# A hybrid decoder step whose weights stream through TensorE: where its side work stands between the weight jobs

## The chip, the core and the metric

The kernel runs on one core of one Trainium2 chip. The metric is the device time of one execution in microseconds (us), as a median over runs. A profiler recorded one further execution, and every duration below comes from that record. Its engines are called PE (TensorE matmul), PEld (TensorE's weight load, which runs beside PE), DVE (VectorE), ACT (ScalarE), POOL (GpSimd) and SP (SyncE, which here only issues DMAs).

## What is computed

One inference step of a one-layer trunk, for 256 prompt tokens and 8 x 4 sample tokens together, 288 columns in all:

```python
x = layer_norm(x)                                   # 2048 features
a_h, a_bg, a_cg, qkv, z, beta, dec, c_u, c_v, gates = split_cols(x @ w_in)
out_a = (a_bg * causal_dwconv(a_cg * a_h)) @ w_a_out
o     = gated_delta_rule(q, k, v, g, beta, state)   # 8 heads, 128 x 128, from silu(conv(qkv))
out_b = (rms_norm(o) * silu(z)) @ w_b_out
out_c = (gelu(c_u) * chunk_spatial_mix(layer_norm(gelu(c_v)))) @ w_c_out
merged = sig(g0) * out_a + sig(g1) * out_b + sig(g2) * out_c
x   = layer_norm(ALPHA * x + merged @ w_o)
ffn = (silu(causal_dwconv(x @ w_up_g)) * (x @ w_up_u)) @ w_down
ple = sigmoid(x @ w_pg) * (p @ w_pe)
y   = layer_norm(ALPHA * x + ffn + ple)
```

The new convolution and delta-rule states are outputs as well. All is float32.

## The kernel before

**Weights and jobs.** All weight matrices are cut into 128 x 128 tiles and laid into one list in the order of use. Eight tiles are a *job*, one 512 KB DMA (`raw`, line 56). ACT copies a job to the rounded type fp32r (`wh`, line 74), DVE subtracts to get the rest (`wl`, line 81), and for each tile PE makes three matmuls of 288 columns (lines 212 to 214): high part of the activations by `wh`, their low part by `wh`, their high part by `wl`. The activations are held as a high and a low part too (`XH` and `XL`, and pairs like it). The list has 614 jobs. `Stream.next` hands out the tiles; when a job starts it runs, in this order, one piece of side work (`pump`), the DMA of a later job, the split of the job two ahead (`wh` on ACT, `wl` on DVE), and then the evacuations that fell due (`post`). In the middle of a job it calls `half`.

**Side work.** `later(fn, lag)` puts a function on a list that `pump` takes from, one per job. If that list is empty, `pump` advances a Python generator, `delta()`, by one step; `delta` is the gated delta rule. A step ends at a `yield`. A plain `yield` means that the next step starts at the next job's start. `yield 1` means that the next step may already run at the coming half. While the q, k and v columns are produced, a job that starts with such an evacuation skips its step. `staged` holds second halves of evacuations, run by the next `post`. `drain()` runs the evacuations, the list and then the generator to its end at once.

**The order of units** (a unit is one 128-row output): c_v, c_u (16 jobs each), q/k/v (48), gate 2 with `wc` (48), mixer A (48), gate 0 with `wa` (48), then `drain()`, z (16 jobs, from job 224), gate 1 with `wb`, `wo`, `wpe`, `wpg`, `wup`/`wdn` twice, and the output norm.

**Inside `delta()`**, for each of four groups of two heads: a step A transposes k, q and v to tokens (line 757) and makes their norms (`ss`, and `rr` by POOL). A step B makes the decays: three DVE operations `dec`, `decT`, `dec`, two exponentials on ACT. It ends with `yield 1`. Step C is one DVE operation, `kh` = k times `rr`. Step D transposes `kh` (line 782). Later a small triangular inverse goes to DRAM (`td`, line 826) and comes back in another shape by four DMAs into a buffer that the trace calls U (line 831). Four steps later DVE makes from it the tiles `T` and `U`, which the next step's matmuls (line 847) read. After the four groups come two passes for the samples, in which `kvd` goes to DRAM and back (line 1055), `son` is scaled, and PE transposes it (line 1074).

**`first()`** begins a run of units on a freshly normalised input: it goes over the 16 slices of features, and for each slice over four or eight accumulators, while `feed` makes the next slices' `XH` and `XL`. It is used for c_v at the start (4 accumulators) and for the first eight `wpg` units (8 accumulators, so that one slice is one job). For `wpg`, each accumulator's evacuation is a sigmoid on ACT into a buffer `u` (four buffers), and `fin`, three DVE operations (`M` times `u`, `t` = `XH` + `XL`, `M` + ALPHA `t`), which a `post()` runs at once.

**At the start** PE makes 40 matmuls on zeros (`warm`, line 255, tile `wz`) while the input arrives and is normalised. The first job is split in two halves (`split0`), lines 456 and 457; `ln.piece(1)` normalises features 512 to 1023 (`yt`, line 128) on DVE.

Of the kernel before, what the change touches and what calls it, by code (L numbers as in the profile page):

```python
# [18 lines left out]
KD = 16  # L19
# [81 lines left out]
def body(tc, I, O):  # L101
# [15 lines left out]
    def tt(out, a, b, op):  # L117
        V.tensor_tensor(out=out, in0=a, in1=b, op=op)  # L118

    def stt(out, a, s, b, op0, op1):  # L120
        V.scalar_tensor_tensor(out=out, in0=a, scalar=s, in1=b, op0=op0, op1=op1)  # L121
# [13 lines left out]
    def mid(ap, n):  # L135
        return ap.unsqueeze(1).to_broadcast([ap.shape[0], n, ap.shape[1]])
# [11 lines left out]
    def acc():  # L148
        return accp.tile([P, 512], F32, name="acc", tag="acc")

    def bank():
        return bgp.tile([P, 512], F32, name="bank", tag="bank")

    def t288(tag, bufs, pl=None):
        return (pl or tmp).tile([P, NT], F32, name=tag, tag=tag, bufs=bufs)

    def short():
        return t288("t", 6)

    def held():  # L160
        return t288("u", 4)

    st = Stream(nc, rawp, whp, wlp, I["wall"], 5, 2)
    deferred = []
    background = [None]
    posted = []
    staged = []
# [4 lines left out]
    def later(fn, lag=1):  # L172
        deferred.append((st.started + lag, fn))

    def pump():
        if deferred:
            if st.started >= deferred[0][0]:
                deferred.pop(0)[1]()
        elif background[0] is not None and not (heavy[0] and pace[0]):
            step()  # L180
# [11 lines left out]
    def flush():  # L192
        post()
        while deferred:
            deferred.pop(0)[1]()

    def drain():
        flush()
        while background[0] is not None:
            pump()  # L200
# [5 lines left out]
    X = (XH, XL)  # L206

    def mm3(key, pair, k, a, start, stop):
        wh, wl = st.next(key)
        xh, xl = pair[0][:, k, :], pair[1][:, k, :]  # L210
        o = a[:, 0:NT]
        PE.matmul(o, lhsT=wh, rhs=xh, start=start, stop=False)  # L212
        PE.matmul(o, lhsT=wh, rhs=xl, start=False, stop=False)  # L213
        PE.matmul(o, lhsT=wl, rhs=xh, start=False, stop=stop)  # L214

    def unit(name, m, pair, nk, evac, k0=0, now=False, a=None):
        a = acc() if a is None else a
        for k in range(nk):
            mm3((name, m, k0 + k), pair, k, a, k == 0, k == nk - 1)
        if now or len(st.order) % JT:  # L220
            evac(a)
        else:
            posted.append(lambda: evac(a))
            heavy[0] = name == "win" and m[0] in (C_QKV, C_QKV + 1024, C_QKV + 2048)

    def post(everything=True):
        late = staged[:]
        staged.clear()
        for f in late:
            f()  # L230
        while posted:
            posted.pop(0)()
        heavy[0] = False
        if everything and staged:
            post()
# [3 lines left out]
    def split_to(hl, i, y):  # L239
        copy(hl[0][:, i, :], y)  # L240
        tt(hl[1][:, i, :], y, hl[0][:, i, :].bitcast(F32), ALU.subtract)
# [10 lines left out]
    def warm(n, w=None):  # L252
        w = bank() if w is None else w
        for _ in range(n):
            PE.matmul(w, lhsT=wz[:, 0:P], rhs=wz, start=True, stop=True)

    def cv(i, n=1):
        return cvec[:, i:i + n]
# [85 lines left out]
    def feed(ln, off, k):  # L344
        if 0 <= k + 2 < KD:
            ln.s3(k + 2, off)
        if 0 <= k + ln.lead < KD and k + ln.lead not in ln.p:
            ln.s1(k + ln.lead, off)
        if 0 <= k + ln.lead - 1 < KD:
            ln.s2(k + ln.lead - 1, off)  # L350

    def first(names, ln, off, evacs, func):
        accs = [acc() if i < 4 else bank() for i in range(len(names))]
        st.late = True
        for k in range(KD):
            if k == KD - 4:
                st.late = False
            if k == KD - 2:
                A.preload_act_table(func)
            for a, (n, m), e in zip(accs, names, evacs):  # L360
                mm3((n, m, k), X, k, a, k == 0, k == KD - 1)
                if k == KD - 1:
                    e(a)
                    if len(names) > 4:
                        post()
            if k in (2, 6):
                ln.piece((k + 6) // 4)
            feed(ln, off, k)
# [46 lines left out]
    for j in range(2):  # L415
        s = BLK[j][0]
# [8 lines left out]
    for j in range(1, 4):  # L425
        st.dma(j)
    nc.sync.dma_start(out=cvec[:, 32:V_N], in_=I["cvec"][:, 32:V_N])
    warm(40)
    xs = M[0:NTS].rearrange("p k t -> p (k t)")[:, 0:16 * P]
    nm = const.tile([NTS, 2], F32, name="nm")  # L430
    A.activation(out=xs, in_=ln.yt[0:NTS, 2, :], func=AF.Identity, scale=-1.0 / 2048, accum_out=nm[:, 0:1])
# [22 lines left out]
    def split0(i):  # L454
        c = slice(i * 4, i * 4 + 4)
        A.activation(out=h0[:, c, :], in_=r0[:, c, :], func=AF.Copy)
        V.tensor_tensor(out=l0[:, c, :], in0=r0[:, c, :], in1=h0[:, c, :].bitcast(F32), op=ALU.subtract)
# [36 lines left out]

    for k in range(-ln.lead, 0):
        feed(ln, V_LNI, k)
        if k == -3:
            split0(1)
        if k == -2:
            st.split(1)  # L500
            ln.piece(1)
    st.subs()
    first([("win", (C_CV, m)) for m in range(4)], ln, V_LNI, [cv_evac(m) for m in range(4)], AF.Gelu_apprx_tanh)
    lstack.close()
    vln.pad(G)
# [175 lines left out]
    def delta():  # L681
# [39 lines left out]
        def D(tag, dt=F32, n=4):  # L721
            return dp.tile([P, n, P], dt, name=tag, tag=tag)
# [16 lines left out]
        for g in range(4):  # L739
# [33 lines left out]
            tt(Dm, Dm, mid(mk["mbS"], 4), ALU.add)  # L773
            A.activation(out=dT, in_=dT, func=AF.Exp)
            A.activation(out=Dm, in_=Dm, func=AF.Exp, scale=-1.0)
            yield 1
            kh = D("kh")
            tt(kh, kb, last(rr[:, 0:4], P), ALU.mult)
            yield
# [51 lines left out]
                nc.sync.dma_start(out=ex[:, u], in_=td[8 * u:8 * u + 8])  # L831
            yield 1
            yield 1
            yield 1
            yield 1
            U, T = D("U", F32R), D("T", F32R)
            for m, X2 in enumerate((T, U)):
                tt(X2.rearrange("p u (r c) -> p u r c", c=16),
# [1 line left out]
                   bd4.rearrange("p u (r c) -> p u r c", c=16), ALU.mult)  # L840
            B = D("B", F32R)
            G.tensor_tensor(out=B, in0=L, in1=mid(mk["m16"], 4), op=ALU.mult)
            yield
            for s in (16, 32, 64):
                w = b4(bank())
# [33 lines left out]
            for c in range(2):  # L879
                us = (c, 2 + c)  # L880
                if c:
# [4 lines left out]
                    for hh, u in enumerate(us):  # L886
                        h = 2 * g + hh
# [16 lines left out]
                else:  # L904
                    S2 = D("S2", n=2)
                    for hh in range(2):
                        h = 2 * g + hh
# [63 lines left out]
        for p in range(2):  # L971
# [7 lines left out]
            tt(Dm, Dm, mk["mbS4"], ALU.add)  # L979
            A.activation(out=dT, in_=dT, func=AF.Exp)  # L980
            A.activation(out=Dm, in_=Dm, func=AF.Exp, scale=-1.0)
            yield 1
            kb = bank()
            for i, src in enumerate((ks, qs, vs)):
                PE.transpose(kb[:, i * P:(i + 1) * P], src, ident)
# [67 lines left out]
            G.memset(kv3[3 * NTS:P], 0.0)  # L1053
            for i in range(3):
                G.dma_start(out=kv3[i * NTS:(i + 1) * NTS], in_=kvd.rearrange("(h t) d -> t h d", t=NTS))
            yield 1
            w = bank()
            PE.matmul(w[:, 0:P], lhsT=dT, rhs=vn, start=True, stop=True)
            tt(on, on, w[:, 0:P], ALU.add)
# [31 lines left out]
            for hl in range(4):  # L1091
                h = 4 * p + hl
# [17 lines left out]
        ds.close()  # L1110

    background[0] = delta()
    next(background[0])

# [60 lines left out]
        unit("win", (C_G, m), X, KD, gate_evac(gs))  # L1175
        unit("wa", m, YB, H, out_acc(m))

    drain()
    ng = cv(V_NB)

    def z_evac(h):
        def e(a):
            sz = held()
            A.activation(out=sz, in_=a[:, 0:NT], func=AF.Silu)
            y = short()
            stt(y[:, 0:NTP], QF[:, h, :], ng, sz[:, 0:NTP], ALU.mult, ALU.mult)
            stt(y[:, NTP:NT], SF[:, 0, h, :], ng, sz[:, NTP:NT], ALU.mult, ALU.mult)
            split_to(YB, h, y)
        return e

    for h in range(H):
        unit("win", (C_Z, h), X, KD, z_evac(h))
    post()
    astack.close()
# [20 lines left out]
    Y = l1p.tile([P, KD, NT], F32, name="Y")  # L1215
# [151 lines left out]

    def pg_evac(m):
        def e(a):
            s = held()  # L1370
            A.activation(out=s, in_=a[:, 0:NT], func=AF.Sigmoid)

            def fin():
                tt(M[:, m, :], M[:, m, :], s, ALU.mult)
                t = short()
                tt(t, XH[:, m, :].bitcast(F32), XL[:, m, :].bitcast(F32), ALU.add)
                stt(M[:, m, :], t, ALPHA, M[:, m, :], ALU.mult, ALU.add)
            staged.append(fin)
        return e

    first([("wpg", m) for m in range(8)], ln1, V_LN1, [pg_evac(m) for m in range(8)], AF.Sigmoid)
    l1stack.close()
    gstack.close()
    ystack.close()
    for m in range(8, KD):
        unit("wpg", m, X, KD, pg_evac(m))

    fstack = ExitStack()
    fp = pool(fstack, "fp")
# [196 lines left out]
```

## Time and profile before

| | |
|---|---|
| median of 3 runs | 2123.72 us (2121.94 to 2125.68) |
| profiled execution: its own time, its span | 2124.1 us, 2122.3 us |
| granted TensorE clock, mean over the span | 0.996 |
| PE busy | 2095.5 us, 99% |
| DVE busy | 1221.9 us, 58% |
| ACT busy | 961.2 us, 45% |
| POOL busy | 231.5 us, 11% |
| DMA | 346.37 MB, mean 163 GB/s; the main queue takes 46.7% of 16 engines' span |

Times in the trace count from the start of the span. A row of the timeline has the start, the duration, the engine, the line of the code, the operation, output and inputs, shape and count. The bracket at its end says how long the engine stood idle just before, and which engine's work let it go on. The table of waits sums those brackets.

### The profile page before, as it was taken

The page shows a single profiled execution, that of the slowest core. Times are in us where ns is not written, and L with a number is a line of the kernel's source. Part 1 is how long each engine was busy: PE and PEld are TensorE (multiplying, and loading weights), DVE is VectorE, ACT ScalarE, POOL GpSimd, SP SyncE. Part 2 cuts the span into 40 slices and gives each one's busy share as a digit, 9 for nine tenths or more (in the row PEclk, how much of TensorE's full clock was granted, in tenths as well). Part 3 has the DMA queues.
Part 4 walks back from the last instruction along what each step waited for, and adds up shares of the span by engine and source line. Part 5 has one row for each costly group of instructions (what it writes and reads, how often), then busy time and mean ns, then how long its engine had stood idle before and what let it go on. Part 6 is the DMA issues. An engine that isn't in the chain of part 4 may idle for free.

```text
span 2122.3 us, 38082 instructions
## 1 busy us (share of the span) xinstructions
PE 2095.5 (99%) x15708; PEld 2078.4 (98%) x15708; DVE 1221.9 (58%) x1761; ACT 961.2 (45%) x1470; POOL 231.5 (11%) x446
## 2 busy tenths in 40 slices
PE   9999999999999999999999999999999999999998
PEld 8999999999999999999999999999999999999998
DVE  6757866566565556545577565555544455555444
ACT  6446544343434445443445634444433344444333
POOL 2112321001101122000000201111100011111000
PEclk9999999999999999999999999999999999999999
DMA  6454544444345466454544444445454454544542
GB/s 241 144 169 159 165 158 143 152 139 154 124 153 183 139 214 213 161 171 162 189 159 149 160 149 166 167 162 169 161 168 163 165 168 162 168 163 165 167 160 105
DMA packets 101533, 346.37 MB, mean 163 GB/s; under 512 B 16352, under 2 KB 16912, under 8 KB 101200
## 3 DMA queue, kind: packets, MB, share of 16 engines
q1 hardware_dynamic: 97888, 331.90, 46.7%
q0 software_dynamic: 3472, 12.05, 1.8%
q8 instruction: 123, 2.02, 0.4%
q14 instruction: 50, 0.41, 0.1%
HBM read 335.22 MB, written 8.67 MB: 162 GB/s over the span
## 4 chain that ended last, share of the span: by engine, by line
PE 93%; DVE 3%; issue 2%; ACT 1%; POOL 1%; DMA 0%; POOLq 0%; DVEq 0%; ACTq 0%
PE acc L212 30%; PE acc L214 29%; PE acc L213 29%; DVE wl L81 1%; PE bank L213 0%; PE bank L212 0%; PE bank L214 0%; PE bank L290 0%; PE bank L1017 0%; ACT wh L74 0%; DVE yt L128 0%; DMA kvd<-skv 0%; PE bank L847 0%; PE bank L858 0%; PE bank L325 0%
## 5 line engine op out<-in xcount | busy, mean ns | idle before, releaser
L81 DVE TENSOR_TENSOR wl<-raw,wh 128x1024 fp32r<-128x1024 f32 x611 | 752.9, 1233 | 732.7 <-ACT wh L74 731.9
L212 PE MATMUL acc<-XH,wh 128*128 128x288 f32 x3480 | 1040.5, 299 | 0.0
L213 PE MATMUL acc<-XL,wh 128*128 128x288 f32 x3480 | 1028.8, 296 | 0.5 <-DVE XL L118 0.5
L214 PE MATMUL acc<-XH,wl 128*128 128x288 f32 x3480 | 1025.6, 295 | 3.4 <-DVE wl L81 3.4
L74 ACT ACTIVATE wh<-raw 128x1024 fp32r<-128x1024 f32 x611 | 645.7, 1058 | 745.9 <-PE acc L213 602.3
L214 PEld LDWEIGHTS acc<-XH,wl 128*128 128x128 f32 x3480 | 657.2, 189 | 3.6 <-DVE wl L81 3.6
L213 PEld LDWEIGHTS acc<-XL,wh 128*128 128x128 f32 x3480 | 656.1, 189 | 1.2 <-DVE XL L118 0.9
L212 PEld LDWEIGHTS acc<-XH,wh 128*128 128x128 f32 x3480 | 655.1, 188 | 0.6
L214 PE MATMUL acc<-HH,wl 128*128 128x288 f32 x688 | 204.7, 297 | 0.0
L212 PE MATMUL acc<-HH,wh 128*128 128x288 f32 x688 | 204.5, 297 | 0.0
L213 PE MATMUL acc<-HL,wh 128*128 128x288 f32 x688 | 203.6, 296 | 0.0
L213 PEld LDWEIGHTS acc<-HL,wh 128*128 128x128 f32 x688 | 129.8, 189 | 0.0
L212 PEld LDWEIGHTS acc<-HH,wh 128*128 128x128 f32 x688 | 129.5, 188 | 0.2
L214 PEld LDWEIGHTS acc<-HH,wl 128*128 128x128 f32 x688 | 129.2, 188 | 0.0
L381 POOL COPY nhf<-ext 128x2 f32<-128x2 f32 x43 | 41.8, 972 | 698.1 <-ACT ext L113 698.1
L212 PE MATMUL acc<-YH,wh 128*128 128x288 f32 x384 | 114.6, 298 | 0.0
L213 PE MATMUL acc<-YL,wh 128*128 128x288 f32 x384 | 113.3, 295 | 0.0
L214 PE MATMUL acc<-YH,wl 128*128 128x288 f32 x384 | 112.9, 294 | 0.0
L121 DVE SCALAR_TENSOR_TENSOR cvo<-ext,cvec,cvo 128x304 f32<-128x304 f32 (+1 forms) x174 | 95.8, 551 | 12.7 <-ACT cvo L387 9.1
L212 PE MATMUL acc<-MH,wh 128*128 128x288 f32 x256 | 76.2, 298 | 0.0
L213 PE MATMUL acc<-ML,wh 128*128 128x288 f32 x256 | 75.5, 295 | 0.0
L214 PE MATMUL acc<-MH,wl 128*128 128x288 f32 x256 | 75.3, 294 | 0.0
(417 smaller groups left out, 1789.2 us busy)
## 6 DMA issues: line engine op xcount, KB each, us to landing
raw<-in_wall SPq DMA_DIRECT2D x611, 512.0 KB, 3.3
st<-in_sd POOLq DMA_DIRECT2D x8, 512.0 KB, 5.6
out_nds<-st SPq DMA_DIRECT2D x8, 512.0 KB, 3.4
yt<-in_x SPq DMA_DIRECT2D x9, 256.0 KB, 3.6
out_y<-vo SPq DMA_DIRECT2D x7, 288.0 KB, 2.3
gbr<-in_lnc POOLq DMA_DIRECT2D x1, 1024.0 KB, 6.2
dec<-gd POOLq DMA_DIRECT2D x8, 128.0 KB, 4.2
M<-in_wall SPq DMA_DIRECT2D x2, 512.0 KB
```

What stands on the lines that cost most here:

```text
L74: self.nc.scalar.activation(out=h, in_=r, func=AF.Copy)
L81: self.nc.vector.tensor_tensor(out=l, in0=r, in1=h.bitcast(F32), op=ALU.subtract)
L121: V.scalar_tensor_tensor(out=out, in0=a, scalar=s, in1=b, op0=op0, op1=op1)
L212: PE.matmul(o, lhsT=wh, rhs=xh, start=start, stop=False)
L213: PE.matmul(o, lhsT=wh, rhs=xl, start=False, stop=False)
L214: PE.matmul(o, lhsT=wl, rhs=xh, start=False, stop=stop)
L381: G.tensor_copy(out=dst[:, 0:r], in_=e[:, NTP:NTP + r])
```

## The change

Seven edits:

- In `delta()`, step B ends with a plain `yield` (line 774 after), and so do the step before the samples' transposes (979) and the one that issues the samples' `kvd` DMAs (1053). The steps behind them no longer run at a half.
- Of the four half steps between the DMAs into the buffer U and the step that makes `T` and `U`, two are left; one half step is put behind that step.
- In `first()`, the `post()` after each of eight evacuations is gone. The sigmoids of the eight shared accumulators go to `Y[:, m, :]`, a tile that is free by then, and their `fin`s go on the list of `later`, due one per job. The stacks that hold `Y` are closed after the other eight `wpg` units instead of before.
- `drain()` stands in front of the fifth z unit instead of the first.
- `warm(40)` becomes `warm(48)`.
- `split0(1)` comes one slice later, behind the `XL` of slice 0.
- `ln.piece(1)` comes one slice later too.

```diff
@@ first
                 if k == KD - 1:
                     e(a)
-                    if len(names) > 4:
-                        post()
@@ start
-    warm(40)
+    warm(48)
...
     for k in range(-ln.lead, 0):
         feed(ln, V_LNI, k)
-        if k == -3:
+        if k == -2:
             split0(1)
-        if k == -2:
             st.split(1)
+        if k == -1:
             ln.piece(1)
@@ delta, step B
             A.activation(out=Dm, in_=Dm, func=AF.Exp, scale=-1.0)
-            yield 1
+            yield
             kh = D("kh")
@@ delta, behind the four DMAs into U
                 nc.sync.dma_start(out=ex[:, u], in_=td[8 * u:8 * u + 8])
             yield 1
             yield 1
-            yield 1
-            yield 1
             U, T = D("U", F32R), D("T", F32R)
...
             G.tensor_tensor(out=B, in0=L, in1=mid(mk["m16"], 4), op=ALU.mult)
+            yield 1
             yield
@@ delta, samples
             A.activation(out=Dm, in_=Dm, func=AF.Exp, scale=-1.0)
-            yield 1
+            yield
             kb = bank()
...
                 G.dma_start(out=kv3[i * NTS:(i + 1) * NTS], in_=kvd.rearrange("(h t) d -> t h d", t=NTS))
-            yield 1
+            yield
             w = bank()
@@ z
-    drain()
...
     for h in range(H):
+        if h == 4:
+            drain()
         unit("win", (C_Z, h), X, KD, z_evac(h))
@@ wpg
-            s = held()
+            s = Y[:, m, :] if m < 8 else held()
             A.activation(out=s, in_=a[:, 0:NT], func=AF.Sigmoid)
...
-            staged.append(fin)
+            if m < 8:
+                later(fin, 1 + m)
+            else:
+                staged.append(fin)
...
     first([("wpg", m) for m in range(8)], ln1, V_LN1, [pg_evac(m) for m in range(8)], AF.Sigmoid)
+    for m in range(8, KD):
+        unit("wpg", m, X, KD, pg_evac(m))
+    while deferred:
+        deferred.pop(0)[1]()
     l1stack.close()
     gstack.close()
     ystack.close()
-    for m in range(8, KD):
-        unit("wpg", m, X, KD, pg_evac(m))
```

Three places show how the order of instructions moves. The first is DVE at the decays and at `kh` of the last group of heads (`R` closes step A; `ext`, `cvo` and `t` are evacuations of mixer A, `YL` the second half of one). Before:

```order
L118 TENSOR_TENSOR R<-bank,bg_g 128x512
L81 TENSOR_TENSOR wl<-raw,wh 128x1024
L118 TENSOR_TENSOR ext<-acc,u 128x256
L118 TENSOR_TENSOR ext<-acc,u 128x8x4
L121 SCALAR_TENSOR_TENSOR cvo<-ext,cvec,cvo 128x304 x2
L118 TENSOR_TENSOR dec<-dec,dtok 128x512
L118 TENSOR_TENSOR decT<-dec,mall 128x512
L118 TENSOR_TENSOR dec<-dec,mall 128x512
L81 TENSOR_TENSOR wl<-raw,wh 128x1024
L118 TENSOR_TENSOR kh<-bank,rr 128x512
L118 TENSOR_TENSOR kh<-kh,dtok 128x512
L81 TENSOR_TENSOR wl<-raw,wh 128x1024
```

The same place with the change:

```order
L118 TENSOR_TENSOR R<-bank,bg_g 128x512
L81 TENSOR_TENSOR wl<-raw,wh 128x1024
L118 TENSOR_TENSOR t<-acc,cvo 128x256
L118 TENSOR_TENSOR t<-acc,cvo 128x32
L118 TENSOR_TENSOR dec<-dec,dtok 128x512
L118 TENSOR_TENSOR decT<-dec,mall 128x512
L118 TENSOR_TENSOR dec<-dec,mall 128x512
L81 TENSOR_TENSOR wl<-raw,wh 128x1024
L118 TENSOR_TENSOR YL<-t,YH 128x288
L118 TENSOR_TENSOR kh<-bank,rr 128x512
L81 TENSOR_TENSOR wl<-raw,wh 128x1024
L118 TENSOR_TENSOR kh<-kh,dtok 128x512
```

A whole job's `wl` now stands between the first `kh`, which step D's transposes read, and the second, which comes after them. On PE the distance from step A's transposes to those of `kh` grows from 2 jobs to 3 in this group (and in the two before it; in the first group from 4 to 6). All that follows in `delta()` comes later by the same amounts: the last matmuls of the sample passes stand at job 223 instead of 216, still one job ahead of z.

The second place is DVE where `T` and `U` of the third group are made (`U_5716` and `U_5796` are the buffer that the four DMAs fill; the lines `U<-U,bank` and `T<-T,bank` follow the first matmuls on them). Before:

```order
L121 SCALAR_TENSOR_TENSOR cvo<-ext,cvec,cvo 128x304 x2
L81 TENSOR_TENSOR wl<-raw,wh 128x1024
L118 TENSOR_TENSOR T<-U_5716,mall 128x512
L118 TENSOR_TENSOR U<-U_5716,mall 128x512
L81 TENSOR_TENSOR wl<-raw,wh 128x1024
L118 TENSOR_TENSOR t<-acc,cvo 128x256
L118 TENSOR_TENSOR t<-acc,cvo 128x32
L118 TENSOR_TENSOR U<-U,bank 128x512
```

With the change:

```order
L121 SCALAR_TENSOR_TENSOR cvo<-ext,cvec,cvo 128x304 x2
L81 TENSOR_TENSOR wl<-raw,wh 128x1024 x2
L118 TENSOR_TENSOR t<-acc,cvo 128x256
L118 TENSOR_TENSOR t<-acc,cvo 128x32
L118 TENSOR_TENSOR T<-U_5796,mall 128x512
L118 TENSOR_TENSOR U<-U_5796,mall 128x512
L81 TENSOR_TENSOR wl<-raw,wh 128x1024
L118 TENSOR_TENSOR YL<-t,YH 128x288
L81 TENSOR_TENSOR wl<-raw,wh 128x1024
L118 TENSOR_TENSOR U<-U,bank 128x512
```

`T` and `U` are now one `wl`, so one job, further ahead of the matmuls that read them; against the DMAs that fill the buffer they come one job sooner.

The third place is DVE at the end of the shared `wpg` units. Before, eight `fin`s stand behind each other; these are the last two of them:

```order
L118 TENSOR_TENSOR M<-M,u 128x288
L118 TENSOR_TENSOR t<-XH,XL 128x288
L121 SCALAR_TENSOR_TENSOR M<-t,M 128x288
L118 TENSOR_TENSOR M<-M,u 128x288
L118 TENSOR_TENSOR t<-XH,XL 128x288
L121 SCALAR_TENSOR_TENSOR M<-t,M 128x288
L81 TENSOR_TENSOR wl<-raw,wh 128x1024 x4
```

With the change:

```order
L81 TENSOR_TENSOR wl<-raw,wh 128x1024 x2
L118 TENSOR_TENSOR M<-M,Y 128x288
L118 TENSOR_TENSOR t<-XH,XL 128x288
L121 SCALAR_TENSOR_TENSOR M<-t,M 128x288
L81 TENSOR_TENSOR wl<-raw,wh 128x1024
L118 TENSOR_TENSOR M<-M,Y 128x288
L118 TENSOR_TENSOR t<-XH,XL 128x288
L121 SCALAR_TENSOR_TENSOR M<-t,M 128x288
L81 TENSOR_TENSOR wl<-raw,wh 128x1024
```

Each `fin` now has a `wl` behind it, and from the fifth on some jobs hold two: one from `Y` and one from a later unit's `u`.

## The prediction

> **What bounds the kernel now.** I read the page's busy times first, then the table of waits of PE, then stretches of the span, and last the timeline around each long wait. Of the two lines below, the first has each engine's busy time, its share of the span and its instructions, the second the main DMA queue's packets, MB and share of 16 engines' time.
>
> ```profile
> PE 2095.5 (99%) x15708; PEld 2078.4 (98%) x15708; DVE 1221.9 (58%) x1761; ACT 961.2 (45%) x1470; POOL 231.5 (11%) x446
> ...
> q1 hardware_dynamic: 97888, 331.90, 46.7%
> ```
>
> Of two stretches: length, then busy time of PE, PEld, DVE, ACT and POOL, granted clock, DMA share, GB/s.
>
> ```profile
> 22.00:1000.00 978.00, 964.50 (x7320) 959.26 (x7319) 606.59 (x963) 456.66 (x726) 131.68 (x228) 1.00 0.49 162
> 1000.00:2100.00 1100.00, 1095.86 (x8204) 1094.40 (x8203) 588.58 (x739) 482.30 (x707) 84.36 (x188) 1.00 0.48 162
> ```
>
> PE is the bound, and the weight stream fills about half of what the DMA engines have. Between 22 and 1000 us PE stands idle for 978.00 - 964.50 = 13.5 us, from 1000 to 2100 us for 4.1 us. An edit that leaves PE's matmuls as they are can gain there only what it takes from these 17.6 us, and outside them something at the cold start. The table of waits says whose they are (who waits and for what; us in total, times, longest):
>
> ```profile
> PE bank L782 <- DVE kh L118: 8.6, 3, 4.3
> PE acc L214 <- DVE wl L81: 3.4, 1, 3.4
> PE bank L847 <- DVE U L118: 2.7, 3, 1.2
> PE bank L325 <- DVE yt L128: 1.8, 3, 1.5
> ...
> PE bank L1074 <- DVE son L126: 0.7, 2, 0.6
> ...
> PE acc L213 <- DVE XL L118: 0.5, 1, 0.5
> ...
> PE bank L873 <- DVE W L118: 0.3, 1, 0.3
> ```
>
> Four of these rows (782, 214, 847, 1074) hold 8.6 + 3.4 + 2.7 + 0.7 = 15.4 us, each in front of a matmul whose input is made by DVE in a step that the change moves. PE waits in program order, so nothing else runs under such a wait, and the wait is worth its full length unless something else is late behind it.
>
> **`kh` behind a full step.** The rows are DVE and PE in the second, third and fourth group; the first group shows no wait.
>
> ```profile
> 346.25 0.68 DVE L118 TENSOR_TENSOR kh<-bank,rr 128x512 f32<-128x512 f32 x1
> ...
> 347.08 0.63 PE L782 MATMUL bank<-ident,kh 128*128 128x128 f32 x4 [2.08 <-DVE kh L118]
> ...
> 457.86 0.68 DVE L118 TENSOR_TENSOR kh<-bank,rr 128x512 f32<-128x512 f32 x1
> ...
> 458.69 0.63 PE L782 MATMUL bank<-ident,kh 128*128 128x128 f32 x4 [2.13 <-DVE kh L118]
> ...
> 565.31 0.52 DVE L118 TENSOR_TENSOR ext<-acc,u 128x256 f32<-128x256 f32 x2
> 566.56 1.10 DVE L121 SCALAR_TENSOR_TENSOR cvo<-ext,cvec,cvo 128x304 f32<-128x304 f32 x2 [0.73 <-ACT cvo L387]
> 567.58 0.68 DVE L118 TENSOR_TENSOR dec<-dec,dtok 128x512 f32<-128x512 f32 x1
> ...
> 572.50 0.68 DVE L118 TENSOR_TENSOR kh<-bank,rr 128x512 f32<-128x512 f32 x1
> ...
> 573.33 1.09 PE L782 MATMUL bank<-ident,kh 128*128 128x128 f32 x4 [4.35 <-DVE kh L118]
> ```
>
> With the change PE runs one more job between its arrival and the transposes. A job lasts 3.16 us (the distance of two `wl` below, 1214.13 and 1217.29). The arrivals are 347.08 - 2.08 = 345.00, 456.56 and 568.98, so `kh` has until 348.16, 459.72 and 572.14. `kh` ends now at 346.93, 458.54 and 573.18. In the second group it has 1.2 us to spare, in the third 1.2 us less one `M` operation that the order puts ahead of it (an estimate of 0.45 us from its 0.45 us row in the sums below). In the fourth it would be 1.0 us late, but the two `ext` and `cvo` that held `dec` up from 565.31 to 567.58 are no longer its neighbours. Two short `t` and one `YL` are, which I put at 0.4 to 0.45 us each by that same row, about 1.3 us. So it comes at 573.18 - 2.27 + 1.3 = 572.2, late by 0.1. What goes: all of 8.6 at best; 8.6 - 1.0 - 1.0 = 6.6 if the fourth keeps its neighbours' cost and the third loses as much again. I take 8.3, near the upper end, because both nearest rows clear the bound by 1.2 us.
>
> What is late next: the `wl` just ahead of `kh` ends where `kh` starts, at 346.25, and is read at the third matmul after 348.16. The second `kh` has no reader on PE for several jobs. The exponentials stay where they are. All the later steps of `delta()` move by one job per group and by up to a job per sample pass; they are the same instructions, and the order ends them at job 223, before z starts.
>
> **`T` and `U` one job sooner.** The rows: the four DMAs into the buffer (issue start and total), their time to landing, the first of the two operations, PE, and one `wh` from elsewhere.
>
> ```profile
> 379.10 1.75 SPq L831 DMA_DIRECT2D U<-td  x4
> ...
> DMA to landing us min/median/max: 2.0/2.8/4.1
> ...
> 386.81 0.68 DVE L118 TENSOR_TENSOR T<-U,mall 128x512 fp32r<-128x512 f32 x1
> ...
> 388.24 0.63 PE L847 MATMUL bank<-U,B 128*128 128x128 f32 x4 [0.38 <-DVE U L118]
> ...
> 1216.19 1.06 ACT L74 ACTIVATE wh<-raw 128x1024 fp32r<-128x1024 f32 x1 [2.10 <-PE bank L213]
> ```
>
> PE gets them a job earlier against a lateness of at most 1.2 us, so 2.7 goes. The price is on DVE: `T` would now start about 386.81 - 3.16 = 383.65, and the last of the DMAs, issued about 380.4 (three quarters through 1.75 us), lands between 382.4 and 384.5. DVE may thus stand up to 0.9 us in front of `T`, and the next `wl` is behind it. A `wl` is made two jobs ahead, 6.3 us, of which it and its `wh` need some 2.3 us (1.06 + 1.23), so 0.9 us reaches nobody. Bounds: 1.5 to 2.7; I take 2.7. SP and its queue keep their order here.
>
> **The eight sums.** DVE around the end of the shared units:
>
> ```profile
> 1214.13 1.23 DVE L81 TENSOR_TENSOR wl<-raw,wh 128x1024 fp32r<-128x1024 f32 x1 [1.61 <-ACT wh L74]
> 1217.29 1.23 DVE L81 TENSOR_TENSOR wl<-raw,wh 128x1024 fp32r<-128x1024 f32 x1 [1.94 <-ACT wh L74]
> 1218.43 0.45 DVE L118 TENSOR_TENSOR M<-M,u 128x288 f32<-128x288 f32 x1
> ...
> 1227.90 0.46 DVE L121 SCALAR_TENSOR_TENSOR M<-t,M 128x288 f32<-128x288 f32 x1
> 1228.28 3.49 DVE L81 TENSOR_TENSOR wl<-raw,wh 128x1024 fp32r<-128x1024 f32 x3
> ```
>
> From 1218.43 to 1228.28 DVE does nothing but the 24 operations of eight `fin`s, 9.85 us, 1.23 us each, while three `wl` queue up behind them. That is the 3.4 us wait of line 214. Spread out, the densest two jobs hold two `wl` (1.16 us each in the row of three) and three `fin`s: 2.3 + 3.7 = 6.0 us against 6.32 us of PE time. It fits, with two jobs of lead to absorb a burst. The sigmoids no longer wait for one of four `u` buffers. Gain 3.4; lower bound 2.4 if ACT's eight sigmoids put off the first `wh`.
>
> **Samples, z, start.** The 0.7 us before line 1074 goes for the same reason as at `kh`: half a job, 1.6 us, more room against a longest wait of 0.6. I take 0.6, bounds 0 to 0.7. `drain()` finds an empty generator in both places: 0. If the steps moved past job 224 its cover would be gone and they would run bare on PE; the order shows one job in hand.
>
> At the start the clock decides. The first rows are PE and DVE, the last four a PE row and stretches with PE's busy time and, third from the end, the granted clock:
>
> ```profile
> 10.27 1.24 PE L255 MATMUL bank<-wz 128*128 128x512 bf16 x5
> 13.43 1.95 PE L325 MATMUL bank<-ident,yt 128*128 128x128 f32 x11 [1.52 <-DVE yt L128]
> ...
> 16.03 1.52 DVE L128 TENSOR_SCALAR yt<-yt,lnmv,lnrs 128x512 f32<-128x512 f32 x3
> 17.48 0.43 DVE L118 TENSOR_TENSOR XL<-t,XH 128x288 fp32r<-128x288 f32 x1
> 17.84 0.56 DVE L128 TENSOR_SCALAR t<-bank,cvec 128x288 f32<-128x288 f32 x1
> 18.97 0.84 PE L325 MATMUL bank<-ident,yt 128*128 128x128 f32 x3
> ...
> 22.00 0.49 PE L325 MATMUL bank<-ident,yt 128*128 128x128 f32 x3
> ```
>
> ```profile
> 14.00:14.50 0.50, 0.50 (x5) 0.50 (x6) 0.47 (x1) 0.50 (x2) 0.50 (x2) 1.00 0.95 385
> 14.50:15.00 0.50, 0.50 (x5) 0.50 (x4) 0.46 (x1) 0.50 (x3) 0.50 (x2) 0.53 1.07 430
> ...
> 21.00:21.50 0.50, 0.50 (x5) 0.50 (x4) 0.50 (x2) 0.00 (x0) 0.00 (x0) 0.65 1.02 418
> ```
>
> The clock falls to half at 14.5, three us after the last zero matmul, and is back by 21.5. Eight more of them, at 1.24 / 5 = 0.25 us or a little less, run to about 13.4, into the 1.5 us in which PE waits for `yt`, so they cost nothing. The first `XL` comes earlier by the half `wl` it overtakes, which ends the 0.5 us wait. But `yt`, needed by the transposes at 18.97, now stands behind the second `XL` and a `t`: its end goes from 17.55 to about 18.6, plus a short wait for the `wh` half that also moved, an estimate of 0.5, so 19.1, and PE waits there instead. With the old clock nothing is gained: 0, or 0.1 lost. If the clock holds, the twelve matmuls between the two rows of transposes take 12 x 3.16 / 24 = 1.6 us instead of 22.00 - 19.8 = 2.2 or more, and the transposes 0.5 instead of 0.8: a gain of about 1. Worst, PE's new pause from about 17 to 19 brings a later stretch of half clock like the one seen, 6.8 us long; if 3.4 us of it fall on matmuls, 1.7 us are lost. I take a gain of 0.7, as more activity right before 14.5 speaks for a clock that holds. [...]
>
> **Sum.** 8.3 + 2.7 + 3.4 + 0.6 + 0.7 = 15.7 us, off the profiled execution's own 2124.1 us: 2108.4 us. That execution lies 0.4 us above the median of the runs shown, 2123.72, well inside their spread.
>
> **Rivals.**
> (1) The waits move instead of going: the same steps, now one to seven jobs later, meet other evacuations, as the fourth group met `ext` and `cvo` and waited 4.35 where the others waited 2.1. For it speaks that margins of 0.1 to 1.2 us are small; against it that behind line 847 only one line of a group waits at all (873, 0.3 us). If half of the gain comes back: 2124.1 - 7.9 = 2116.2.
> (2) Nothing changes, because the stream or another engine takes over as bound when PE stops pausing. DVE at 58% and the queue at 46.7% speak against it. 2123.7.
> (3) Slower: `T` stands at the head of DVE's queue before its DMAs have landed, and every `wl` behind it is late. PE feels it from 6.3 - 2.3 = 4.0 us of lateness on, so from a landing 4 us after 383.65, near 7 us after the last issue; the longest in the trace is 4.1. To eat the gain and 5 us more, each of four groups would have to be late by about 4 + 5.2 us. 2129.
>
> **How the numbers follow.** The forecast has 0.82, rival (1) 0.13, (2) 0.03, (3) 0.02. A measurement of this kernel can tell about 0.2%, 4.2 us, from no change; the first two cases lie beyond that: faster 0.95, same 0.03, slower 0.02. All upper bounds give 8.6 + 2.7 + 3.4 + 0.7 + 1.0 = 16.4, so 2107.7, and the runs spread by 2 us below their median's neighbours: low end 2105.5. All lower ones give 6.6 + 1.5 + 2.4 + 0 - 1.7 = 8.8, so 2115.3: high end 2115, which takes in part of rival (1).
>
> **What would show it.** In the changed kernel's waits: the rows of `kh`, `U`, `son` and of `wl` at line 214 gone or under half a us each; PE idle from 22 to 1000 us near 2 us. At the start: clock 1.00 across 14.5 to 21. Against me would be a new row for `wl`, `wh` or `T` of over 2 us, or clock 0.5 after 17 us. The prediction is wrong if PE's idle time between 22 and 2100 us stays above 9 us, or if PE's busy time grows.

## Result and the profile after

The changed kernel takes 2104.87 us (median of 4 runs, 2104.77 to 2106.45) against 2123.71 us of the kernel before on the same chip (4 runs, 2121.94 to 2125.68): ratio 0.9913, 95% interval 0.9896 to 0.993. It is faster, as forecast, but by 3.5 us more than the 2108.4 us forecast and 0.6 us below the low end of the range. The unaltered changed kernel run again beside the last experiments gave 2105.09 us (0.9913, 0.9898 to 0.9928).

The page of the changed kernel, first part, in the same columns as before:

```profile
PE 2090.3 (99%) x15715; PEld 2074.6 (99%) x15716; DVE 1224.5 (58%) x1761; ACT 960.6 (46%) x1470; POOL 236.1 (11%) x446
```

PE's busy time fell by 5.2 us although its matmuls are the same but for eight more on zeros. The prediction had said that PE can gain only from its idle time. The same stretch as before (length, busy times of PE, PEld, DVE, ACT, POOL, clock, DMA share, GB/s):

```profile
22.00:1000.00 978.00, 976.97 (x7432) 973.89 (x7431) 617.55 (x976) 460.96 (x732) 136.53 (x228) 1.00 0.50 165
```

Here 13.5 us of idle time became 1.0. From 1000 to 2087 us, before PE runs out of work in either kernel, it went from 4.1 to 0.75 us. PE's whole table of waits over 0.3 us:

```profile
PE bank L325 <- DVE yt L128: 3.2, 4, 2.1
PE bank L255 <- DVE wz L250: 1.2, 1, 1.2
PE acc L212 <- ACT M L113: 0.7, 1, 0.7
PE acc L213 <- DVE XL L118: 0.6, 1, 0.6
PE bank L290 <- DVE M L118: 0.5, 1, 0.5
PE bank L290 <- ACT gv L489: 0.5, 1, 0.5
PE bank L870 <- DVE W L118: 0.3, 1, 0.3
```

The rows of `kh`, `U`, `wl` and `son` are gone and no new row stands between 22 and 2087 us. The first row grew: `yt`, at the start, from 1.8 to 3.2 us.

Where the time went is read from the start of the same job in both profiled executions. The last column is after minus before, and the difference of two rows is the gain of the stretch between them (worked out from the records of the weight matmuls):

| start of job | before, us | after, us | after - before | what lies in the stretch that ends here |
|---|---|---|---|---|
| 2 | 26.08 | 28.37 | +2.30 | the start |
| 88 | 330.29 | 332.56 | +2.27 | nothing that the change moves |
| 100 | 374.91 | 374.92 | +0.01 | `kh` of the second group |
| 130 | 486.52 | 483.60 | -2.92 | `kh` of the third group, one `U` |
| 160 | 603.15 | 592.28 | -10.88 | `kh` of the fourth group, one `U` |
| 225 | 847.92 | 833.61 | -14.31 | one `U`, the sample passes |
| 342 | 1225.72 | 1211.42 | -14.30 | nothing |
| 344 | 1237.29 | 1217.82 | -19.47 | the eight sums |
| 613 | 2103.11 | 2083.61 | -19.50 | the rest |

Two things stand out: the fourth group and the sums gave more than their waits (7.96 us for waits of 4.35 and 1.19; 5.17 us for a wait of 3.4), and the start, forecast as a gain of 0.7, cost 2.3.

**The clock explains most of the first.** I had read the clock only at the start. These stretches of 0.2 us of the kernel *before* lie inside the wait for the last `kh`, at the end of the half clock behind it (the third number from the end is the granted clock), and behind the wait for `wl`:

```profile
570.70:570.90 0.20, 0.00 (x0) 0.00 (x0) 0.00 (x0) 0.20 (x1) 0.00 (x0) 1.00 0.00 0
570.90:571.10 0.20, 0.00 (x0) 0.00 (x0) 0.00 (x0) 0.20 (x1) 0.00 (x0) 0.50 0.00 0
577.60:577.80 0.20, 0.20 (x3) 0.20 (x3) 0.09 (x1) 0.00 (x0) 0.00 (x0) 0.69 0.00 0
...
1229.60:1229.80 0.20, 0.20 (x1) 0.20 (x2) 0.20 (x1) 0.00 (x0) 0.00 (x0) 0.68 0.00 0
1232.80:1233.00 0.20, 0.20 (x3) 0.20 (x3) 0.00 (x0) 0.00 (x0) 0.00 (x0) 0.50 0.25 102
1233.00:1233.20 0.20, 0.20 (x3) 0.20 (x3) 0.00 (x0) 0.00 (x0) 0.00 (x0) 0.79 1.35 287
```

The clock drops at 570.9 us, while PE waits, and is back at 577.7. That is 6.83 us, twice the 3.41 us for which it stays down behind the `wl` wait (1229.67 to 1233.08); 3.41 us is called a window below. PE resumes at 573.3, so 4.4 us of matmuls ran at half clock. What that costs is read from the start times of the weight matmuls, before the wait and behind it:

```profile
564.16 0.29 PE L213 MATMUL acc<-XL,wh 128*128 128x288 f32 x1
564.29 0.29 PE L214 MATMUL acc<-XH,wl 128*128 128x288 f32 x1
...
575.18 0.44 PE L213 MATMUL acc<-XL,wh 128*128 128x288 f32 x1
575.42 0.44 PE L214 MATMUL acc<-XH,wl 128*128 128x288 f32 x1
```

One follows the other after 0.24 us instead of 0.133, so 45% of the time at half clock is lost: 2.0 us here, and 1.5 us of the 3.4 us at half clock behind the `wl` wait. That is about 3.5 us that no table of waits shows; it is booked as PE's busy time. In the changed kernel the clock is 1.00 from 25.4 us to the end of the weights.

**The start.** DVE, POOL and PE of the changed kernel (in brackets the wait and who ended it):

```profile
17.93 2.99 DVE L128 TENSOR_SCALAR yt<-yt,lnmv,lnrs 128x512 f32<-128x512 f32 x3
18.08 0.94 POOL L276 MEMSET yt<- 32x1024 f32 x1
19.06 1.13 POOL L277 MEMSET yt<- 64x1024 f32 x1
19.45 0.30 PE L325 MATMUL bank<-ident,yt 128*128 128x128 f32 x1 [2.08 <-DVE yt L128]
...
20.53 0.77 PE L325 MATMUL bank<-ident,yt 128*128 128x128 f32 x2 [0.78 <-DVE yt L128]
```

```profile
21.50:22.00 0.50, 0.50 (x6) 0.50 (x5) 0.50 (x2) 0.43 (x1) 0.00 (x0) 0.96 1.04 406
22.00:22.50 0.50, 0.50 (x4) 0.50 (x3) 0.50 (x3) 0.00 (x0) 0.00 (x0) 0.50 0.96 389
...
25.00:25.50 0.50, 0.50 (x4) 0.50 (x4) 0.50 (x2) 0.34 (x1) 0.00 (x0) 0.62 0.83 320
```

`yt` starts at 17.93 instead of 16.03 us, as the prediction's order said. But its three operations take 2.99 us instead of 1.52: they now run beside GpSimd's memsets (the same two began at 18.68 us before, after `yt` was done). PE waits 2.1 + 0.8 us, and then the clock falls to half for 3.4 us.

### The profile page after: what moved, and what is told of

The parts are those of the page before. It is cut to its first block, busy times and chain, and to the rows that moved or that the text cites. A ratio compares the mean times of both kernels' runs of the same rounds, so it can differ in the third digit from the quotient of the medians.

```text
span 2103.1 us, 38091 instructions
## 1 busy us (share of the span) xinstructions
PE 2090.3 (99%) x15715; PEld 2074.6 (99%) x15716; DVE 1224.5 (58%) x1761; ACT 960.6 (46%) x1470; POOL 236.1 (11%) x446
## 4 chain that ended last, share of the span: by engine, by line
PE 98%; DVE 1%; ACT 0%; POOL 0%; issue 0%; POOLq 0%; DVEq 0%; ACTq 0%
PE acc L212 31%; PE acc L214 30%; PE acc L213 30%; PE bank L1014 1%; PE bank L255 1%; PE bank L213 0%; PE bank L212 0%; PE bank L214 0%; DVE yt L128 0%; PE bank L290 0%; PE bank L855 0%; PE bank L755 0%; PE bank L325 0%; PE bank L853 0%; PE bank L844 0%; PE bank L1094 0%
```

## Experiments

Each kernel's time is a median over 4 to 11 runs, with its ratio to the kernel before on the same chip. "Theory A" and "B" in the expectations are, in general, my reading after the result and its rival.

**E1: the `kh` edit alone.** The kernel before with one line changed, in step B:

```diff
             A.activation(out=Dm, in_=Dm, func=AF.Exp, scale=-1.0)
-            yield 1
+            yield
             kh = D("kh")
```

> Only the plain yield behind step B, on the kernel before. Theory A: a pause of PE that fills more than about half of one window of 3.41 us halves the clock for whole windows, so the 4.35 us wait in the fourth group also cost 2.2 us at half clock (570.9 to 577.7, of which PE worked from 573.3). Then all three kh waits go (8.6 us), PE's busy time falls by about 2.2 us, the clock stays 1.00 across that place: 2123.7 - 10.8 = 2112.9 us. Theory B: a wait is worth its own length and the surplus of the change lies elsewhere: PE's busy time stays at 2095.5 within 1 us, 2115.1 us.

Measured: 2108.95 us (2108.39 to 2109.96), ratio 0.9931 (0.9918 to 0.9943), 14.9 us less than the 2123.82 us beside it. Both theories forecast too small a gain. In its profile `kh` waits for nothing, the clock stays at 1.00 where `kh` was, and a second row has shrunk too:

```profile
PE acc L214 <- DVE wl L81: 3.4, 1, 3.4
PE bank L325 <- DVE yt L128: 1.8, 3, 1.5
PE bank L847 <- DVE U L118: 1.2, 3, 0.4
```

`U` went from 2.7 to 1.2 us without its own edit: a job later, other evacuations stand ahead of it on DVE. The small wait for `W` (0.3 us before) is gone as well. From job 42 to job 225, the stretch of `delta()`, the profiled execution is 13.4 us shorter than that of before: 8.6 (idle) + 2.0 (clock) + 1.5 (`U`) + 0.6 (three restarts, below) + 0.5 (`W` and its restart) = 13.2 us. The other 1.5 us lie ahead of job 42, in code that the edit leaves alone: at the start the clock was at half for 3.4 us in this execution and for 6.8 in the profile of before. That part is luck of the two executions.

**E2: the eight sums alone.** The kernel before with the edits of `first()` and `pg_evac` and the moved stacks:

```diff
-                    if len(names) > 4:
-                        post()
...
-            s = held()
+            s = Y[:, m, :] if m < 8 else held()
...
-            staged.append(fin)
+            if m < 8:
+                later(fin, 1 + m)
+            else:
+                staged.append(fin)
```

> Only the eight sums one per job, on the kernel before. Theory A: the 3.4 us wait filled a whole window, and 1.7 us more went at half clock from 1229.7 to 1233.1: 2123.7 - 5.1 = 2118.6 us, and no stretch at half clock there. Theory B: 2123.7 - 3.4 = 2120.3 us.

Measured: 2119.06 us (2116.38 to 2120.26), 0.9979 (0.9969 to 0.9989): 4.8 us gained. The interval holds both theories; the profile decides for A, since jobs 342 to 344 gained 5.17 us, exactly what the full change gained there, and the clock stays at 1.00. This execution also shows that the clock's fall is a matter of phase. Group two's `kh` waits as it did before, yet here the clock falls, and in before's profile it didn't:

```profile
345.52 1.09 PE L780 MATMUL bank<-ident,kh 128*128 128x128 f32 x4 [2.08 <-DVE kh L118]
...
345.20:345.60 0.40, 0.08 (x1) 0.11 (x2) 0.17 (x1) 0.04 (x1) 0.00 (x0) 0.83 0.00 0
345.60:346.00 0.40, 0.40 (x3) 0.40 (x4) 0.00 (x0) 0.00 (x0) 0.00 (x0) 0.50 0.16 51
348.60:349.00 0.40, 0.40 (x4) 0.40 (x4) 0.40 (x1) 0.00 (x0) 0.00 (x0) 0.65 0.00 0
```

From job 88 to job 100 this execution takes 46.14 us, that of before 44.62. Two us of idle time are thus enough to lose 1.5 us more, in some executions.

**E3: the clock alone, in the last `kh` wait.** The kernel before, with matmuls on zeros in the pause; the wait itself stays:

```diff
-            kb = b4(bank())
+            kw = bank()
+            if g == 3:
+                warm(19, kw)
+            kb = b4(kw)
```

> The kernel before, with 19 matmuls on zeros (0.216 us each, 4.1 us) just ahead of the fourth group's transposes of kh: kh is as late as before, but PE does not pause. Theory A: the clock stays 1.00 there and 2.2 us are saved although nothing was made earlier: 2121.5 us; kh still ends near 573.2. Theory B: pausing and working on zeros cost the same: 2123.7 us, or a little more if the zeros outlast the wait.

Measured: 2121.99 us (2119.44 to 2123.05), 0.9988 (0.9979 to 0.9997). The fillers and the transposes behind them:

```profile
566.43 4.28 PE L255 MATMUL bank<-wz 128*128 128x512 bf16 x19
...
570.10 0.69 DVE L118 TENSOR_TENSOR kh<-bank,rr 128x512 f32<-128x512 f32 x1
...
570.84 0.66 PE L785 MATMUL bank<-ident,kh 128*128 128x128 f32 x4
```

`kh` comes no sooner, PE's pause is filled with useless work, and jobs 130 to 160 still run 2.05 us shorter: theory A, with 2.2 us expected. What the `kh` wait cost beyond its length is nearly all the clock.

**E4: the start put back.** The changed kernel with the start of the kernel before:

```diff
-    warm(48)
+    warm(40)
...
-        if k == -2:
+        if k == -3:
             split0(1)
+        if k == -2:
             st.split(1)
-        if k == -1:
             ln.piece(1)
```

> The changed kernel with the start as it was (40 zero matmuls, split0(1) and ln.piece(1) at their old slices), all else kept. Theory A: the start edits lose 2.3 us, as the third job starts 2.3 us later with them: 2104.9 - 2.3 = 2102.6 us. Theory B, the prediction's: they gain 0.7 us, so this gives 2105.6 us.

Measured: 2101.59 us (2100.73 to 2103.09), 0.9897 (0.9883 to 0.991), 3.3 us below the changed kernel. The start edits are a loss (theory A): every run of this kernel is faster than every run of the changed one, and E9 to E11 show it again on one chip. In the profile `yt` takes 1.52 us again, PE waits 1.0 us for `XL`, and the clock is 1.00 throughout.

**E5: `piece(1)` alone put back** (one slice earlier; the other start edits stay):

```diff
             st.split(1)
-        if k == -1:
             ln.piece(1)
```

> The changed kernel with only ln.piece(1) back at its old slice (48 zero matmuls and the later split0(1) stay). Theory A: the loss at the start is PE waiting for yt, which the change put behind an XL and a t: the 2.9 us of waits in front of the transposes go, and with them the pause that halves the clock: 2104.9 - 2.3 to 3.3 = 2101.6 to 2102.6 us. Theory B: the 48 zero matmuls or the later split half are to blame: it stays at 2104.9 us.

Measured: 2101.61 us (2101.32 to 2104.9), 0.9894 (0.9879 to 0.9909). The whole loss sits in this one edit, and the other two start edits together gain nothing that can be measured. `yt` takes 1.44 us from 16.94, and PE's wait for it is

```profile
PE bank L325 <- DVE yt L128: 0.8, 3, 0.5
```

**E6: 48 zeros in front of the old start.** E4 with `warm(48)` kept.

> The changed kernel with the start's old order, but 48 zero matmuls instead of 40. Theory A: they hold the clock through the first jobs whatever the window's phase, so it never falls before 20 us; where it fell at 40 a run lost 1.5 to 3 us, where it did not nothing is gained: median 2100.7 to 2101.6 us and no run above 2102. Theory B: they delay the first transposes: 2102 us or more.

Measured: 2101.32 us (2100.49 to 2102.4), 0.9889 (0.9875 to 0.9904). Not told apart from E4: the eight more zeros are worth nothing that can be measured, as long as `yt` is early. (One of its four runs was above 2102, against what theory A said, and its profile has an `XL` wait of 0.7 us at 33 us that E4's lacks with the same code around it; E7's has it too.)

**E7: E4 without the `T`/`U` edit** (four half steps ahead of `U` again, none behind):

```diff
             yield 1
             yield 1
+            yield 1
+            yield 1
             U, T = D("U", F32R), D("T", F32R)
...
-            yield 1
             yield
```

> As e4 (changed kernel, old start), but T and U made at their old step. Theory A: moving kh shifted all later steps by a job per group and gave T and U other neighbours on DVE, so their waits are then 1.2 us in all, as in e1: 2101.6 + 1.2 = 2102.8 us. Theory B: their edit is worth the 2.7 us of the profile before: 2104.3 us.

Measured: 2102.95 us (2102.09 to 2104.81), 0.9899 (0.9883 to 0.9916), 1.4 us above E4. The runs of the two overlap, and each was taken on another chip (the ratios are 0.9899 and 0.9897), so the profiles decide: from job 42 to job 225 this execution is 1.45 us longer than E4's. `U` waits 1.2 us in all, as in E1: theory A. Putting the edit in takes 2.0 us from the stretch with these waits (jobs 88 to 225) and gives back 0.54 us before it, where the wait for `W` returns. Of the 2.7 us that the prediction booked for this edit, it earns about half; the other half came with `kh`.

**E8: the memsets moved away from `yt`.** The changed kernel with `yt` still late, and the memsets of the next norm's padding on DVE and a job later:

```diff
-    vln.pad(G)
+    later(lambda: vln.pad(V))
```

> The changed kernel with the memsets of the second norm's padding on DVE some jobs later instead of on POOL beside the yt operations. Theory A: POOL's memsets slowed yt (2.99 us for three operations against 1.52 before): yt takes 1.5 us again, PE's wait there falls from 2.9 to about 1.4 us: 2103.4 us, or 2101.7 if the clock then stays up. Theory B: yt is slow for another reason: it takes 3.0 us and the time stays at 2104.9 us.

Measured: 2101.68 us (2101.26 to 2102.48), 0.9891 (0.9877 to 0.9906), theory A with a clock that stays. DVE and PE:

```profile
17.90 1.44 DVE L128 TENSOR_SCALAR yt<-yt,lnmv,lnrs 128x512 f32<-128x512 f32 x3
...
18.59 1.14 PE L325 MATMUL bank<-ident,yt 128*128 128x128 f32 x3 [1.26 <-DVE yt L128]
```

`yt` starts at the same place as in the changed kernel (17.90 against 17.93) and takes half as long, 1.44 us against 2.99: the memsets doubled it. Taken one by one, the records of the changed kernel tell more: each of the two 128x512 operations ends 0.28 us after the memset beside it has ended (19.30 after 19.02, 20.47 after 20.19), and the same holds in E9 (19.58 after 19.29, 20.75 after 20.46). So the operation seems to wait for the memset's end rather than to run more slowly throughout.

**E9: the changed kernel again**, beside E10 to E12.

> The changed kernel once more, unaltered, so that the three kernels sent with it have it beside them on the same chip. Theory A (the start costs about 3.3 us against a start that keeps the clock): 2104 to 2106 us. Theory B (the 3.3 us between it and the kernels with another start lie between the sets of runs, not in the start): 2101 to 2103 us, the same as its neighbours.

Measured: 2105.09 us (2103.52 to 2105.69): theory A. Its fastest run is also the only one whose mean clock was 1.000; the three others, at 0.998 to 0.999, took 2104.83 to 2105.69.

**E10: zeros in the pause for `yt`.** The changed kernel with eight zero matmuls ahead of the late transposes:

```diff
             ps = bank()
+            if k == 4 and fill:
+                warm(fill.pop(), ps)
             for j, (s, w) in enumerate(BLK):
                 PE.transpose(ps[:, s:s + P], self.yt[:, j, k * P:(k + 1) * P], ident)
```

> The changed kernel with eight matmuls on zeros (about 0.25 us each, 2.0 us in all) on TensorE ahead of the transposes that wait 2.08 us for yt at 17.4 to 19.45 us. Nothing else is changed, so the transposes come no sooner. Theory A (of the start's loss, the half clock that follows the pause holds some 1.7 us and the lateness of yt the rest): the clock stays at 1.00 behind the pause and the time falls by 1.5 to 1.7 us against the changed kernel beside it. Theory B (the lateness of yt is the whole loss): no difference, or 0.1 us longer.

Measured: 2103.13 us (2102.95 to 2103.9), 0.9905 (0.9891 to 0.992), 2.0 us below E9; from job to job 1.60 us. The clock stayed:

```profile
22.00:24.00 2.00, 2.00 (x18) 2.00 (x17) 2.00 (x5) 1.25 (x2) 0.00 (x0) 1.00 0.99 333
```

Theory A. Against E5 the changed start loses 3.85 us at job 2; 1.6 us of it is the clock and 2.25 the lateness itself. E8 gives the split of the lateness: 1.55 us from the memsets, 0.7 from the two operations that `yt` stands behind.

**E11: `piece(1)` back and the memsets moved** (E5 and E8 together).

> The changed kernel with ln.piece(1) back one slice earlier, and the memsets of the other norm's padding moved from GpSimd to VectorE and to a later job. Each alone gave 2101.6 to 2101.7 us. Theory A (both take away the same loss, the lateness of yt with its half clock, and the memsets cost 0.5 us elsewhere): 2101.0 to 2101.6 us. Theory B (two separate losses of 3.2 us): 2098.5 us.

Measured: 2100.73 us (2100.43 to 2101.28), 0.9894 (0.9879 to 0.9908): theory A, 0.3 us below its range. Both had removed the same loss; the 0.7 us more comes from jobs 10 to 20, where the 0.5 us wait for `gv` is gone. This is the fastest kernel of the study, 4.4 us below the changed kernel beside it.

**E12: the samples' edit put back.** E5 with both sample steps ending at a half again:

```diff
             A.activation(out=Dm, in_=Dm, func=AF.Exp, scale=-1.0)
-            yield
+            yield 1
             kb = bank()
...
-            yield
+            yield 1
             w = bank()
```

> The changed kernel with ln.piece(1) back and without the edit of the two sample steps (both end at a half again). Theory A (the prediction's 0.6 us for the wait of line 1074): 0.5 to 0.7 us above the kernel with ln.piece(1) back (2101.6 us), and that wait in the table of waits again. Theory B (behind the later kh the wait is gone without the edit): no difference.

Measured: 2102.98 us (2102.61 to 2103.61), 0.9905 (0.9888 to 0.9921), 1.4 us above E5; 2.05 us from job 160 to 225 of the two profiles. Both theories missed. Its waits, and the stretch of jobs 160 to 225 in E5 and in E12:

```profile
PE bank L1070 <- DVE son L126: 0.6, 2, 0.3
...
PE bank L995 <- PE acc L214: 0.4, 1, 0.4
...
PE bank L995 <- DVE skv L126: 0.3, 1, 0.3
```

```profile
588.42:829.76 241.34, 241.10 (x1838) 239.76 (x1837) 147.02 (x234) 116.14 (x200) 48.34 (x54) 1.00 0.53 182
```

```profile
588.42:831.81 243.39, 241.92 (x1839) 239.72 (x1838) 146.51 (x234) 116.40 (x200) 46.17 (x54) 1.00 0.54 183
```

The edit removes two kinds of wait, not one: at line 995 (999 in the kernel before) as well as at 1070 (1074). And four waits with 1.2 us more idle time (1.47 against 0.24) make PE's *busy* time 0.8 us longer, at the same clock and with as many matmuls. The records show how: a weight matmul lasts 0.29 us in them, and the next one starts 0.13 us after it. In an unbroken stream the last 0.16 us of a record are covered by the next; ahead of a wait they are not, and the idle row begins only at their end. So a wait costs its idle row and, here, about 0.2 us more (0.82 / 4), which I call a restart.

## Why the prediction was partly right

Direction and mechanism held: all four rows went, and none took their place. The margins that the prediction worked out were met: `kh` of the fourth group, put at 572.2 us, comes so that its transposes wait no more, though the room is small (DVE and PE of the changed kernel):

```profile
573.15 0.69 DVE L118 TENSOR_TENSOR kh<-bank,rr 128x512 f32<-128x512 f32 x1
...
574.08 0.60 PE L780 MATMUL bank<-ident,kh 128*128 128x128 f32 x4
```

With `kh` done at 573.84 that leaves 0.24 us. Rival (1), that half of the gain comes back, is refuted by the table of waits, and (2) by the time. (3), the late DMAs into `U`, did occur on a small scale (DVE stood about 1.5 us in front of one `T`), and no PE wait followed.

The step that failed is the sentence "the wait is worth its full length unless something else is late behind it". With it fails the bound drawn from it, that such an edit can gain in that stretch only what it takes from 17.6 us of idle time. A wait is worth more than its length, for two reasons that its row doesn't show: the clock and the restart. By terms:

| term | predicted gain | measured | what the prediction left out |
|---|---|---|---|
| `kh` | 8.3 | 11.2 | 2.0 clock (E3: 2.05), 0.6 for three restarts; no remainder of 0.3 |
| `T`, `U` | 2.7 | 3.3 | 0.6 for three restarts; half of the 2.7 is due to the `kh` edit (E1, E7) |
| eight sums | 3.4 | 5.2 | 1.5 clock (E2), the restart |
| samples | 0.6 | 2.1 | line 999 and the restarts (E12) |
| start | 0.7 | -2.3 | `yt` slowed by the memsets, and the clock (E8, E10) |
| sum | 15.7 | 19.5 | the profiled executions differ by 19.5 at job 613 |

The measured column for `kh` and `U` is their idle rows plus restarts at 0.2 us and the clock, which agrees with the jobs of the table above (2.26, 2.93, 7.96 and 3.43 us for the stretches that hold them and the samples: 16.6 against 11.2 + 3.3 + 2.1 = 16.6). The start's 2.3 is measured against one execution of the kernel before, which itself had lost time to 6.8 us of half clock there; with the old start and a clock that held, E4's median lies 3.3 us below the changed kernel.

The second failed step is the start. Its lateness was seen: `yt` was to end at about 19.1 us and PE to wait for it. It ended at 20.9, because I costed its three operations by their 1.52 us at the old place, and did not look at what POOL does at the new one: before, its memsets began at 18.68 us, 1.1 us after `yt` had ended. Then I took a gain of 0.7 on the guess that the clock would hold, though the prediction named the pause of 17 to 19 us as what might drop it, at 1.7 us: that worst case was what happened in both profiled executions of the changed kernel (E9 is the other), at 1.6 us (E10). Of the prediction's signs, the clock of 1.00 from 14.5 to 21 us came true, and so did the one against it, half clock after 17 us. That more activity before 14.5 us holds the clock, the prediction's reason for the 0.7, no run shows: with 40 zeros the clock held as well in E4, and in place of the gain the start lost 2.3 us.

The range failed on its low end: it was all upper bounds plus scatter, and none of the bounds went above the length of a wait. The errors partly cancelled, +6.8 us on four terms against -3.0 on the start; that the total came out only 3.8 us off is luck to that extent.

## What to carry to other kernels

In this kernel a pause of the saturated TensorE cost its idle time, about 0.2 us for the restart (E12, 0.82 us over four waits), and, from about two us of idle time on, with some luck of phase, another 1.5 to 2.5 us at half clock (1.52 in E2, 2.05 by E3, about 2.5 behind E3's `wl` wait): look at the clock around every long wait, not only at the start, and look at PE's busy time when idle time doesn't explain a difference. When work is moved later, list what the *other* engines do at the new place; here the same three DVE operations took 2.99 us beside GpSimd's memsets and 1.44 without them (E8). Where a wait couldn't be removed, zeros on TensorE during it saved the clock's part (2.05 us in E3, 1.60 in E10).

## What was unexpected about the hardware

In the traces the clock changes only at the edges of 3.41 us windows, whose phase against the program differs between executions. In the profile of before it changes at 14.53, 21.35, 570.90, 577.73, 1229.67 and 1233.08 us, which lie 2, 161, 2, 191 and 1 times 3.413 us apart. Counted back from 570.90, one edge lies at 345.62 us, inside the second group's wait for `kh` (345.00 to 347.08); in E2 the edge at 345.46 lies at the end of that wait (343.44 to 345.52). PE's idle time per such window, added up from the records of the profiled executions: two windows with 1.70 us of idle time (before: 454.85 to 458.26; after: 15.14 to 18.55) kept the clock. Windows with 1.79 us (after: 18.55 to 21.96), 1.91 (before: 567.49 to 570.90), 2.03 and 2.56 (E2: 342.05 to 345.46 and 570.74 to 574.15) and 3.29 us (before: 1226.26 to 1229.67) were followed by half clock. One with 1.60 us, at before's start (11.11 to 14.53), which also held many transposes, dropped it too. Two windows stand against a sharp bound: 1.79 us in E2 (567.33 to 570.74) kept the clock, and so did 1.60 us with at least as many transposes at E4's start (11.94 to 15.35). So of the windows listed, those from 1.60 to 1.79 us went both ways, and each with 1.91 us or more was followed by half clock: the bound lies near half a window of idle time here. The cost varies with phase as well: in E3 the `wl` wait of 3.40 us was followed by 5.6 us at half clock instead of 3.4, and jobs 342 to 344 took 12.55 us instead of 11.57. Whether transposes count like other matmuls is not tested, and no run set the length of a pause on purpose, so the bound itself is a reading of these windows, while the cost of a drop is shown (1.52 us in E2, 2.05 in E3, 1.60 in E10).
